# A bank of its own for the state products of a gated delta layer, and two output columns issued after the last head's sums

## The chip, the cores and the metric

One core of a Trainium2 chip runs the whole program. The metric is device time in microseconds (us) of one execution, as a median over several runs.

## What is computed

The program is a small network of three blocks on 512 tokens of width 1024. The change touches the first alone: a gated delta-rule layer with 8 heads of width 128, computed in chunks of 64 tokens. Cut to what matters:

```python
h = modulated_norm(x); proj = h @ w_in            # q, k, v, z: 4 x 8 column blocks of 128
# per head, chunks of 64: solve (I + L) [u, w] = [beta v, beta k exp(g)], L strictly lower triangular
def step(S, inp):                                 # 8 chunks, one after the other
    v_new = u_i - w_i @ S
    o = q_i @ S + a_i @ v_new
    S = S * gl_i + k_i.T @ v_new
    return S, o
o = rms(o) * silu(z)                              # per head
x = x + gate * (o.reshape(T, 8 * 128) @ w_out)    # output projection over all heads
```

Then follow a second attention layer and a third block with attention, an mLSTM and a mixture of experts. All matmuls of projections are done three times with operands split into a high and a low part (`mm3`, lines 106 to 108).

## The kernel before

A scheduler orders each engine's instructions from the program text, with its own estimate of times; each engine then works through its queue strictly in that order. What stands where is therefore read from the built order, and a change in one place can move instructions in others.

**Projections.** `proj_T` makes one column block of 128 outputs for all 512 tokens: per block of 128 inputs three matmuls of 128x512 (L106 to L108). The weights come from memory, ScalarE rounds them to the high part `wh` (L99), and the low part `wl` is subtracted on GpSimd or VectorE (L102). Which of the two is chosen in `wtile` by a running number, `self.uid`, that every buffer request counts up: VectorE where it divides by 9, else GpSimd.

**A head** (`gdn_head`). Its front transposes k and v and builds L. The solve runs five levels; each is a transpose (L611), a product with the masked L (L616; GpSimd makes the mask product `Lm`, L607) and a second product (L621). These, and the products u (L628) and w (L632), go through PSUM bank `v0` or `v1`, by the head's parity. The chain of 8 chunks then works in bank `s0` or `s1`, 512 columns in four quarters: R, the product with the state (L646), is read by VectorE to update u (L647) and by ScalarE to copy the inter-chunk output (L648); pS, the state product (L650), is read by VectorE to make the next state (L655). After the chain come the sums (L658: a product of A and u), the norm over the head (ScalarE, VectorE, GpSimd L123 and L668), transposes of the result (L670) and the product with silu(z) into `oT` (L671), which is split into `oH` and `oL` (L99, L102).

**The output projection** (`residual`) runs in two parts, `EARLY_A`: for all 8 column blocks first the heads 0 to 6 (7 input blocks, 21 matmuls a column), then head 7 alone (3 matmuls a column). After each, VectorE adds the column (L300); after the last part squares are summed for the next norm (L198, L114, a power on GpSimd at L123).

**Beside it.** Rows of the modulation (`ada`) are multiplied and summed in the head loop: the first two on VectorE in one instruction (L173), the others on GpSimd and ScalarE (L176, L177).

Of the kernel before, what the change touches and what calls it, by code (L numbers as in the profile page):

```python
# [19 lines left out]
P = 128  # L20
T = 512
D = 1024
KC = D // P
# [10 lines left out]
class Net:  # L34
# [251 lines left out]
                         w16[0][:, k], w16[1][:, k], k == 0, k == KC - 1)  # L286
        cb(p[:, :NT * 16].rearrange("p (i c) -> p i c", i=NT))

    def residual(self, w, act, gate, x_in, x_out, scratch=None, parts=(slice(0, KC),)):

        nc = self.nc
        held = {}

        def cb(j, p, first, last):
            src = x_in(j) if first else held.pop(j)
            out = x_out[:, j] if last else src
            if gate is None:
                nc.vector.tensor_tensor(out, src, p, op=ALU.add)
            else:
                nc.vector.scalar_tensor_tensor(out, p, gate[:, j:j + 1], src, op0=ALU.mult, op1=ALU.add)  # L300
            held[j] = out
            if last:
                held["sq"] = self.square(out, src if scratch is None else scratch(j), held.get("sq"), nc.vector)
        for ks in parts:
            self.proj_T(w, 0, KC, act, lambda j, p: cb(j, p, ks is parts[0], ks is parts[-1]), ks=ks)
        self.uid += 1
        self.rms = self.mean([held["sq"]], f"x{self.uid}")

# [18 lines left out]
class Gdn(Net):  # L327
# [9 lines left out]
    def gdn(self):  # L337
        nc, tc, a = self.nc, self.tc, self.a
# [4 lines left out]
        with ExitStack() as st:  # L343
# [8 lines left out]
            act = (hH, hL)  # L352
            w = a["w_in_a"]
            rts = ExitStack()
            rt = rts.enter_context(tc.tile_pool(name="g_rt", bufs=1))
            with tc.tile_pool(name="g_t", bufs=2) as tmp, tc.tile_pool(name="g_ada0", bufs=self.A0) as ap0:
# [11 lines left out]
                parts = {}  # L368
# [128 lines left out]
            oH = hp.tile([P, KC, T], F32R, tag="hH", name="oH")  # L497
            oL = hp.tile([P, KC, T], F32R, tag="hL", name="oL")
# [10 lines left out]
            class Out:  # L509

                def __getitem__(_, at):
                    if not x1:
                        x1[0] = self.xtile("x1")
                    return x1[0][at]
            self.residual(a["w_out_a"], (oH, oL), self.mod0[:, 16:24], x_in, Out(), parts=self.EARLY_A)
            x1 = x1[0]
            self.dump("x1", x1)
        return x1
# [7 lines left out]
    def gdn_head(self, hd, h, q, k, v, z, gcol, rows, oT):  # L526
        nc = self.nc
        dcm, strm, lvs, lv0t = self.masks
        mm = nc.tensor.matmul
# [28 lines left out]
        p = self.pg()  # L558
# [6 lines left out]
        A, B = late("A", [NT, P], 3), new("B", [NT, P], 2)  # L565
# [5 lines left out]
        for i2 in range(0, NT, 2):  # L571
            p = self.pg().rearrange("p (i a c) -> p i a c", i=2, a=2)
# [14 lines left out]
        p = self.pg()  # L587
# [5 lines left out]
        p = self.pg()  # L593
# [31 lines left out]
        u = late("u", [NT, P], 2)  # L625
        p = self.pg()
# [3 lines left out]
        p = self.pg()  # L630
# [5 lines left out]

        o = late("ot", [NT, P], 2)
        nc.gpsimd.memset(o[:64, 0], 0.0)
        ps = self.pg(f"s{h % 2}")
        S = None  # L640
        for c in range(T // 64):
            i, b = divmod(c, 2)
            pr, qr = slice(b * 64, b * 64 + 64), slice(64 - b * 64, 128 - b * 64)
            R, pS = ps[:, b * 256:b * 256 + P], ps[:, b * 256 + P:b * 256 + 256]
            if S is not None:
                mm(R, WQ[:, i, b].rearrange("p a c -> p (a c)"), S, start=True, stop=True, skip_group_check=True)  # L646
                nc.vector.tensor_tensor(u[pr, i], u[pr, i], R[pr], op=ALU.subtract)  # L647
                nc.scalar.copy(o[pr, i], R[qr])  # L648
            if c < T // 64 - 1:
                mm(pS, kd[pr, i], u[pr, i], start=True, stop=True, skip_group_check=True)  # L650
                S2 = late(f"S{h % 2}", [P], 2)
                if S is None:
                    nc.vector.tensor_copy(S2, pS)
                else:
                    nc.vector.scalar_tensor_tensor(S2, S, gl[:, c:c + 1], pS, op0=ALU.mult, op1=ALU.add)  # L655
                S = S2
        for i in range(NT):
            mm(ps[:, i * P:(i + 1) * P], A[:, i], u[:, i], start=True, stop=True, skip_group_check=True)  # L658
        nc.vector.tensor_tensor(o, o, v4(ps), op=ALU.add)

        ss = late("ss", [NT], 2)
# [977 lines left out]
```

## Time and profile before

| | |
|---|---|
| median of 3 runs | 2809.9 us (2806.88 to 2825.23) |
| the profiled execution | 2808.36 us, span 2806.6 us |
| TensorE / VectorE / ScalarE / GpSimd busy over the span | 95% / 61% / 43% / 62% |
| granted TensorE clock, mean | 0.983 of full speed |
| first layer | to about 520 us; its head loop from about 60 to 440 us |
| second layer, third block, experts | to about 900, 1510 and 2806 us |

In the rows below, PE is TensorE's matmul, PEld its weight load, DVE VectorE, ACT ScalarE and POOL GpSimd. A timeline row gives start, duration, engine, line, operation, output<-inputs, shape and count; in brackets stands the idle time of the engine before it and what ended it. Equal instructions in a row are merged, and a tile's number is left out, so that heads are told apart by counting in the order of the program. A 128x128 product of 32-bit numbers shows as two matmuls.

### The profile page before, as it was taken

What the parts mean: (1) busy time and instruction counts of PE and PEld (TensorE: products, weight loads), DVE (VectorE), ACT (ScalarE), POOL (GpSimd) and SP (SyncE); (2) the same over time, 40 slices, a digit from 0 to 9 for tenths busy, and PEclk for the clock granted to TensorE, in tenths of its full rate; (3) what the DMA queues carried; (4) which work ended last, traced back from release to release, by engine and by line L of the source; (5) the groups of instructions that cost most, each with busy time, mean ns of one, the idle gap of its engine ahead of it and who ended that gap; (6) DMA issues with size and microseconds to landing.
All of it is one profiled execution on the core that took longest, in us unless ns stands there. A gap on an engine that the chain in (4) does not pass through costs nothing. (4 is left out here: it accounts for less than half of the span.)

```text
span 2806.6 us, 40394 instructions
## 1 busy us (share of the span) xinstructions
PE 2663.2 (95%) x14601; PEld 2262.4 (81%) x14601; DVE 1698.3 (61%) x3092; ACT 1209.0 (43%) x2505; POOL 1735.8 (62%) x1338
## 2 busy tenths in 40 slices
PE   6899998799998999999998999999999999999999
PEld 4787777697776877787777899999999977777777
DVE  7767774614445654222232697798876167678897
ACT  5566663636664454233333333434434333333332
POOL 4799983543232521444365368878788478887886
PEclk9999999899998999999999999999999999999999
DMA  6243331221011111212122478888888889999996
GB/s 241 95 139 121 121 113 32 71 98 61 29 42 50 61 37 55 74 62 75 61 86 87 136 264 292 305 293 317 314 289 309 279 289 333 339 331 334 334 324 226
DMA packets 206793, 499.35 MB, mean 178 GB/s; under 512 B 18304, under 2 KB 106624, under 8 KB 203520
## 3 DMA queue, kind: packets, MB, share of 16 engines
q1 hardware_dynamic: 167856, 359.19, 38.0%
q0 software_dynamic: 36864, 134.23, 13.4%
q10 hardware_dynamic: 1872, 3.33, 0.4%
q8 instruction: 115, 1.88, 0.3%
q14 instruction: 86, 0.70, 0.1%
HBM read 444.26 MB, written 52.43 MB: 177 GB/s over the span
## 5 line engine op out<-in xcount | busy, mean ns | idle before, releaser
L102 POOL TENSOR_TENSOR wl<-wr,wh 128x256 fp32r<-128x256 f32 (+2 forms) x503 | 418.0, 850 | 493.1 <-ACT wh L99 466.0
L102 POOL TENSOR_TENSOR upl<-upr,uph 128x1024 fp32r<-128x1024 f32 x128 | 311.9, 2437 | 97.0 <-ACT uph L99 96.0
L99 ACT ACTIVATE wh<-wr 128x256 fp32r<-128x256 f32 (+2 forms) x556 | 228.4, 445 | 305.0 <-PE pj L107 114.5
L106 PE MATMUL pj<-nH,downh 128*128 128x384 f32 x1024 | 353.4, 345 | 2.4 <-ACT w L1458 1.3
L108 PE MATMUL pj<-nH,downl 128*128 128x384 f32 x1024 | 350.0, 342 | 2.7 <-DVE downl L102 2.7
L107 PE MATMUL pj<-nL,downh 128*128 128x384 f32 x1024 | 349.9, 342 | 0.0
L102 POOL TENSOR_TENSOR downl<-downr,downh 128x1024 fp32r<-128x1024 f32 x96 | 238.1, 2482 | 134.0 <-ACT downh L99 132.9
L1503 PE MATMUL acc<-uph,wwh 128*128 128x512 f32 x768 | 302.4, 399 | 8.9 <-ACT wwh L99 8.9
L1503 PE MATMUL acc<-upl,wwh 128*128 128x512 f32 x768 | 305.8, 398 | 0.0
L99 ACT ACTIVATE downh<-downr 128x1024 fp32r<-128x1024 f32 x128 | 135.4, 1059 | 312.5 <-PE pj L107 188.9
L102 DVE TENSOR_TENSOR wwl<-wo,wwh 128x384 fp32r<-128x384 f32 x128 | 210.8, 1650 | 58.0 <-ACT wwh L99 54.6
L1503 PE MATMUL acc<-uph,wwl 128*128 128x512 f32 x768 | 232.6, 399 | 5.6 <-DVE wwl L102 5.4
L106 PE MATMUL pj<-hH,wh 128*128 128x512 f32 x544 | 219.9, 404 | 2.2 <-ACT mo L1175 1.2
L108 PE MATMUL pj<-hH,wl 128*128 128x512 f32 x544 | 221.1, 407 | 0.3 <-POOL wl L102 0.2
L107 PE MATMUL pj<-hL,wh 128*128 128x512 f32 x544 | 215.3, 396 | 0.0
L99 ACT ACTIVATE uph<-upr 128x1024 fp32r<-128x1024 f32 x128 | 134.8, 1053 | 168.9 <-POOL upl L102 114.2
L106 PEld LDWEIGHTS pj<-nH,downh 128*128 128x128 f32 x1024 | 193.8, 189 | 5.4 <-ACT downh L99 1.6
L108 PEld LDWEIGHTS pj<-nH,downl 128*128 128x128 f32 x1024 | 194.0, 189 | 3.9 <-DVE downl L102 3.6
L107 PEld LDWEIGHTS pj<-nL,downh 128*128 128x128 f32 x1024 | 193.8, 189 | 0.3
L1503 PEld LDWEIGHTS acc<-uph,wwh 128*128 128x128 f32 x768 | 145.1, 189 | 47.7 <-ACT wwh L99 12.8
L1503 PEld LDWEIGHTS acc<-uph,wwl 128*128 128x128 f32 x768 | 145.0, 189 | 42.8 <-DVE wwl L102 7.8
L1503 PEld LDWEIGHTS acc<-upl,wwh 128*128 128x128 f32 x768 | 145.8, 190 | 35.0
(627 smaller groups left out, 6583.2 us busy)
## 6 DMA issues: line engine op xcount, KB each, us to landing
downr<-in_peer_down_j SPq DMA_DIRECT2D x128, 512.0 KB, 4.9
upr<-in_peer_up_j SPq DMA_DIRECT2D x128, 512.0 KB, 5.7
wr<-in_w_in SPq DMA_DIRECT2D x50, 512.0 KB, 4.1
ada<-in_w_ada SPq DMA_DIRECT2D x48, 512.0 KB, 3.8
wait<-w SPq DMA_DIRECT2D x128, 192.0 KB, 4.8
wo<-wait SPq DMA_DIRECT2D x128, 192.0 KB, 5.1
G<-stage SPq DMA_DIRECT2D x24, 1024.0 KB, 7.5
Gt<-G SPq DMA_DIRECT2D x48, 512.0 KB, 8.0
```

Of the source, the lines that this page charges most:

```text
L99: nc.scalar.activation(h, src, AF.Copy)
L102: return (eb or nc.vector).tensor_tensor(l, src, h.bitcast(F32), op=ALU.subtract)
L106: mm(out, lh, rh, start=start, stop=False)
L107: mm(out, lh, rl, start=False, stop=False)
L108: mm(out, ll, rh, start=False, stop=stop)
L1503: mm(po[z][b], lh[:, zs], rh[:, bs], start=False, stop=j == P - 1 and rh is uh and lh is l, skip_group_check=True)
```

## The change

pS moves from the quarter beside R to a bank requested by `self.pg()`, which is the head's own solve bank (`v0` or `v1`), still the tag in force there. R and pS now take the four quarters of their banks in turn. In `residual`, the last two column blocks of the first part are issued behind the last sums matmul of the last head (an edge in TensorE's order, no semaphore); the other six are left to the scheduler.

```diff
-    def residual(self, w, act, gate, x_in, x_out, scratch=None, parts=(slice(0, KC),)):
+    def residual(self, w, act, gate, x_in, x_out, scratch=None, parts=(slice(0, KC),), keep=(0, None)):
...
         for ks in parts:
-            self.proj_T(w, 0, KC, act, lambda j, p: cb(j, p, ks is parts[0], ks is parts[-1]), ks=ks)
+            n = KC - keep[0] if ks is parts[0] else KC
+            self.proj_T(w, 0, n, act, lambda j, p: cb(j, p, ks is parts[0], ks is parts[-1]), ks=ks)
+            if n < KC:
+                with self.tc.issue_after(keep[1].ins):
+                    self.proj_T(w, n, KC - n, act, lambda j, p: cb(n + j, p, ks is parts[0], ks is parts[-1]), ks=ks)
...
-            self.residual(a["w_out_a"], (oH, oL), self.mod0[:, 16:24], x_in, Out(), parts=self.EARLY_A)
+            self.residual(a["w_out_a"], (oH, oL), self.mod0[:, 16:24], x_in, Out(), parts=self.EARLY_A, keep=(2, self.summed))
...
-        ps = self.pg(f"s{h % 2}")
+
+        ps, pS2 = self.pg(f"s{h % 2}"), self.pg()
...
-            R, pS = ps[:, b * 256:b * 256 + P], ps[:, b * 256 + P:b * 256 + 256]
+            R, pS = (p[:, c % 4 * P:c % 4 * P + P] for p in (ps, pS2))
...
-            mm(ps[:, i * P:(i + 1) * P], A[:, i], u[:, i], start=True, stop=True, skip_group_check=True)
+            self.summed = mm(ps[:, i * P:(i + 1) * P], A[:, i], u[:, i], start=True, stop=True, skip_group_check=True)
```

Two things follow from the text without standing in it. The new buffer counts `self.uid` up once more per head, so other weight blocks fall to VectorE: of 556 weight splits 53 stood on VectorE, now 113 do. In the head loop these are 4 column blocks instead of 2, in the third block 10 pairs of blocks instead of 3 (8 splits each); the second pair of the second layer goes from VectorE to GpSimd, with its first split ahead of the rsqrt of that layer's norm. And lines from 289 on have higher numbers in the changed kernel: L646 becomes L652, L650 L656, L658 L664, L670 L676.

First place: TensorE at the end of head 5's chain (tiles s1 and, in the changed kernel, v1; u5, kd5), where head 7's solve (Xv17, Lmv17) begins beside head 6's (v0). Before:

```order
L650 MATMUL s1257_3405<-u5_3389,kd5_3177 128x128 [waits Activation_49]
L616 MATMUL v1314_4286<-Xv17_4278,Lmv17_4284 128x128 [waits Pool_49]
L616 MATMUL v1314_4286<-Xv17_4278,Lmv17_4284 128x128 x3
L611 MATMUL v0290_3877<-c_id_74,Xv06_3868 128x128 [waits DVE_49]
L611 MATMUL v0290_3877<-c_id_74,Xv06_3868 128x128 x3
L646 MATMUL s1257_3405<-S15_3443,WQ5_3231 128x128 [waits DVE_49]
```

Now:

```order
L656 MATMUL v1263_3411<-u5_3394,kd5_3182 128x128 [waits DVE_49]
L652 MATMUL s1262_3410<-S15_3449,WQ5_3236 128x128 [waits DVE_49,Activation_49]
L626 MATMUL v0298_3897<-Yv06_3895,XTv06_3888 128x128 [waits Activation_49]
L626 MATMUL v0298_3897<-Yv06_3895,XTv06_3888 128x128 x3
L621 MATMUL v1321_4293<-Xv17_4285,Lmv17_4291 128x128 x4
L664 MATMUL s1262_3410<-u5_3394,A5_3214 128x128 [waits Activation_49]
```

The state product waits for VectorE in place of ScalarE, and head 7's first solve product stands behind the whole of head 5's chain, just ahead of its sums.

Second place: TensorE around the last head's sums (A7), with columns of the output projection (pj). Before:

```order
L107 MATMUL pj348_4777<-oL_4500,wh348_4798 128x512
L108 MATMUL pj348_4777<-oH_4499,wl348_4799 128x512
L658 MATMUL s1334_4431<-u7_4415,A7_4237 128x128 [waits Activation_49]
L658 MATMUL s1334_4431<-u7_4415,A7_4237 128x128 x3
L106 MATMUL pj348_4777<-oH_4499,wh348_4808 128x512 [waits Activation_49]
```

Now:

```order
L656 MATMUL v1342_4439<-u7_4422,kd7_4212 128x128 [waits DVE_49]
L108 MATMUL pj354_4742<-oH_4507,wl354_4774 128x512 [waits Pool_49]
L652 MATMUL s1341_4438<-S17_4465,WQ7_4266 128x128 [waits DVE_49,Activation_49]
L656 MATMUL v1342_4439<-u7_4422,kd7_4212 128x128 [waits DVE_49]
L652 MATMUL s1341_4438<-S17_4471,WQ7_4266 128x128 [waits DVE_49,Activation_49]
L656 MATMUL v1342_4439<-u7_4422,kd7_4212 128x128 [waits DVE_49]
L652 MATMUL s1341_4438<-S17_4477,WQ7_4266 128x128 [waits DVE_49,Activation_49]
L664 MATMUL s1341_4438<-u7_4422,A7_4244 128x128 [waits Activation_49]
L664 MATMUL s1341_4438<-u7_4422,A7_4244 128x128 x3
L106 MATMUL pj356_4785<-oH_4507,wh356_4786 128x512
```

The last three chunks of the chain have no projection between them any more; the two columns held back (pj356, pj358) follow the sums, 21 and 8 matmuls ahead of the last transposes (L676) and 13 behind them; before, 3 and 21 stood between sums and transposes, and none of the first part behind these.

Third place: GpSimd early in the head loop, with the mask products of head 1 (Xv11, XTv11, Lmv11) and head 0 (Lmv00), weight splits (wl) and a row of the modulation (ada51). Before:

```order
L601 TENSOR_TENSOR Xv11_1194<-B1_1154,c_lv0t_457 128x512
L102 TENSOR_TENSOR wl143_1937<-wr142_0_1933,wh143_1936 128x256
L102 TENSOR_TENSOR wl143_1947<-wr142_0_1933,wh143_1946 128x256
L602 TENSOR_TENSOR XTv11_1195<-Ls1_1192,c_lv0_445 128x512
L607 TENSOR_TENSOR Lmv11_1200<-Ls1_1192,c_lv1_447 128x512
L102 TENSOR_TENSOR wl143_1957<-wr142_0_1933,wh143_1956 128x256
L176 TENSOR_TENSOR ada51_761<-ada51_761,c_rep_118 128x1024
L102 TENSOR_TENSOR wl143_1967<-wr142_0_1933,wh143_1966 128x256
L607 TENSOR_TENSOR Lmv00_763<-Ls0_682,c_lv4_453 128x512
```

Now:

```order
L606 TENSOR_TENSOR Xv11_1195<-B1_1155,c_lv0t_457 128x512
L102 TENSOR_TENSOR wl146_1940<-wr145_0_1936,wh146_1939 128x256
L102 TENSOR_TENSOR wl146_1950<-wr145_0_1936,wh146_1949 128x256
L607 TENSOR_TENSOR XTv11_1196<-Ls1_1193,c_lv0_445 128x512
L612 TENSOR_TENSOR Lmv11_1201<-Ls1_1193,c_lv1_447 128x512
L102 TENSOR_TENSOR wl146_1960<-wr145_0_1936,wh146_1959 128x256
L612 TENSOR_TENSOR Lmv00_763<-Ls0_682,c_lv4_453 128x512
L176 TENSOR_TENSOR ada51_761<-ada51_761,c_rep_118 128x1024
```

Head 0's mask product of the fourth level (Lmv00) now stands ahead of the row of the modulation.

## Rows read from the trace of the kernel before

**Rows 1.** Busy time by stage: stretch, its length, then each engine, TensorE's clock, DMA.

```profile
60.00:440.00 380.00, 355.42 (x2162) 299.51 (x2161) 272.79 (x480) 242.61 (x625) 321.55 (x283) 0.99 0.34 111
...
457.00:469.00 12.00, 8.97 (x26) 6.47 (x27) 5.47 (x15) 3.01 (x11) 3.51 (x4) 0.57 0.00 0
```

**Rows 2.** Timeline, 457 to 461 us: two chunks of the last head's chain.

```profile
457.84 0.48 PE L650 MATMUL s<-u,kd 64*128 64x128 f32 x2 [2.22 <-ACT ot L648]
...
458.77 0.80 PE L646 MATMUL s<-S,WQ 128*128 128x128 f32 x2 [0.44 <-DVE S L655]
...
459.60 0.28 DVE L647 TENSOR_TENSOR u<-u,s 64x128 f32<-64x128 f32 x1 [0.22 <-PE s L646]
459.92 0.26 ACT L648 COPY ot<-s 64x128 f32<-64x128 f32 x1 [2.13 <-DVE u L647]
...
460.23 0.79 PE L650 MATMUL s<-u,kd 64*128 64x128 f32 x2 [0.67 <-ACT ot L648]
```

**Rows 3.** TensorE's waits, 60 to 440 us: total, times, longest.

```profile
PE s L650 <- ACT ot L648: 2.0, 2, 1.4
```

**Rows 4.** Timeline of TensorE: first solve products (L616) and last state products (L650).

```profile
183.95 1.16 PE L616 MATMUL v<-Xv,Lmv 128*128 128x128 f32 x8
...
207.68 0.71 PE L650 MATMUL s<-u,kd 64*128 64x128 f32 x4
...
328.47 1.06 PE L616 MATMUL v<-Xv,Lmv 128*128 128x128 f32 x8
...
344.06 0.48 PE L650 MATMUL s<-u,kd 64*128 64x128 f32 x2
...
423.29 1.16 PE L616 MATMUL v<-Xv,Lmv 128*128 128x128 f32 x8 [0.59 <-POOL Lmv L607]
```

**Rows 5.** Timeline from head 6's sums to the next layer's norm.

```profile
454.25 1.16 PE L658 MATMUL s<-u,A 128*128 128x128 f32 x8
...
463.57 1.22 PE L106 MATMUL pj<-oH,wh 128*128 128x512 f32 x2 [1.08 <-ACT oH L99]
...
494.12 1.05 PE L658 MATMUL s<-u,A 128*128 128x128 f32 x8
...
499.70 1.04 POOL L668 TENSOR_TENSOR ot<-ot,rv_o 128x512 f32<-128x512 f32 x1
...
499.83 0.39 PE L106 MATMUL pj<-oH,wh 128*128 128x512 f32 x1
500.06 0.39 PE L107 MATMUL pj<-oL,wh 128*128 128x512 f32 x1
...
500.79 0.66 PE L670 MATMUL s<-c_id,ot 128*128 128x128 f32 x4
...
504.45 1.41 DVE L300 SCALAR_TENSOR_TENSOR x<-pj,mods,xi 128x512 f32<-128x512 f32 x2 [0.83 <-PE pj L108]
...
513.75 6.36 POOL L102 TENSOR_TENSOR wl<-wr,wh 128x512 fp32r<-128x512 f32 x4 [4.36 <-ACT wh L99]
...
520.08 1.00 POOL L123 TENSOR_TENSOR rv_x<-rv_x,mhalf 128x4 f32<-128x4 f32 x1
```

**Rows 6.** Line L173's instructions from 60 us on; timeline, 129 to 135 us.

```profile
L173 DVE CUSTOM_DVE_ANT_0 ada<-ada,c_rep,cols x2: 1277/5776/10276, 106.8 to 122.5; 128x1024 f32<-128x1024 f32 x2
...
129.39 2.33 POOL L176 TENSOR_TENSOR ada<-ada,c_rep 128x1024 f32<-128x1024 f32 x1
...
134.07 1.11 PE L542 MATMUL n<-c_id,y 128*128 128x128 f32 x4 [8.15 <-DVE vb L591]
```

**Rows 7.** Groups of weight splits, 60 to 440 us; TensorE's waits, 900 to 1510 us.

```profile
L102 POOL TENSOR_TENSOR wl<-wr,wh 128x256 fp32r<-128x256 f32 (+1 forms) x114 | 91.9, 814 | 26.9 <-ACT wh L99 26.0 <-PE s L650 0.6
...
L102 DVE TENSOR_TENSOR wl<-wr,wh 128x256 fp32r<-128x256 f32 x8 | 5.0, 637 | 0.7 <-ACT wh L99 0.7
...
PE l L107 <- POOL wl L102: 0.4, 1, 0.4
```

## The prediction

> **What bounds the kernel now.** I read the page first, then the busy time by stage, then the first layer's waits, and last its timeline, since the change lies there. In the head loop (60 to 440 us) it is busy 355 of 380 us, GpSimd 322, VectorE 273, ScalarE 243 [rows 1]: four engines that feed each other, none with much room. At the end of the layer two heads are left without further input projections, TensorE runs short of work, and from 457 to 469 us the granted clock is 0.57 between its levels of 1.2 and 2.4 GHz, after the idle time before 457.84 [rows 1, 2]. From 469 us on matmuls of the output projection fill every wait. So the change can act on three things: waits inside the state chain, the seam between head 6 and head 7, and the end of the layer. The experts from 1510 us on have the same instructions in nearly the same order, and move only as a block.
>
> One chunk of the chain at 458 us, where nothing else is queued [rows 2]: the product with the state (L646) starts at 458.77; VectorE subtracts it from u at 459.60 for 0.28 us; ScalarE copies the other half at 459.92 for 0.26 us; only then, at 460.23, comes the next state product (L650). It needs u alone, but the trace names ScalarE's copy as its releaser, because both products stand in one bank. At 457.84 the same wait had cost 2.22 us.
>
> **The change part by part.** All sums go against the profiled run, 2808.4 us (span 2806.6). The median of the runs shown is 2809.9, 1.5 us above it and within their scatter.
>
> (a) *State product in the v bank.* In the order its wait changes from ScalarE to VectorE (first place shown). In the step above u ends at 459.88 and a release takes some 0.05 us (copy end 460.18, product 460.23), so a bare step falls by 0.30 us. The next L646 now waits for the copy, which has a whole state update to finish in. 48 such steps would be 14.4 us if all lay on the path; none if projections fill them. As idle TensorE time named after that copy the trace shows 2.0 us in the head loop [rows 3] and 2.22 + 0.67 us in the two steps of rows 2. I take -4 (0 to -14).
>
> (b) *The seam of heads 6 and 7.* Before, head 6's sums (L658) start at 454.25, after the last product of head 7's solve, and the output projection, which needs head 6's normalised output, resumes at 463.57, waiting for its split [rows 5]: 9.3 us with little for TensorE. Now chain 6 is done earlier and its sums stand ahead of head 7's last solve product and of its u and w, so about half of the wait runs under work that has to be done anyway. -5 (0 to -9.3).
>
> (c) *The v bank is held longer.* Head h+2 solves in the bank where head h's state products now stand until its chain ends. Before, head 2's first solve product is at 183.95 and head 0's last state product at 207.68 (with one of head 1), an overlap of 24 us that is no longer allowed; head 5 against head 3 overlaps by 16 us (328.47, 344.06); head 7 starts at 423.29, with no overlap left [rows 4]. TensorE's order fills the shift with projection columns, as long as there are some. By head 7 that cover is nearly gone: head 7's solve now stands behind all of head 5's chain (first place shown), and by counting rows some 3 us more matmul work is ahead of it. Lower bound 0, upper bound the 16 us of head 5 less 14 half steps at 0.30, thus 12. Row 423.29 (no overlap) is nearer to what decides: +4.
>
> (d) *Two columns behind the sums.* Before, 24 matmuls at 0.23 us from start to start (499.83, 500.06) lie between the last sums, 494.12, and the transposes, 500.79, and cover the norm, which ends with the product at 499.70 [rows 5]. Now 29 do, 6.7 us, still enough. But the columns held back are missing ahead of the sums: the last steps stand bare in the order (second place shown). A bare step is 0.93 us (457.84 to 458.77) plus 1.16 (458.77 to 459.88 and a release), 2.1 us. Three of them are 6.3 us with 1.6 us of matmuls, so 4.7 us idle. In return 13 matmuls, 3.0 us, move from before the transposes to after them, where they cover the way from the transposes to the first finished column: before 3.66 us (500.79 to 504.45), now some 0.7 + 3.0 + 0.9 = 4.6. Transposes 4.7 - 3.0 = 1.7 later, then 0.9: +2.6. If the bare steps hide in slack won at (b), it is -2.1; I keep +2.6.
>
> (e) *The rsqrt of the next norm.* On GpSimd four weight splits of the second layer, 6.36 us, stand before it and push it to 520.08 [rows 5]. Now a fifth (1.59 us) stands there, because the running number moved that block from VectorE to GpSimd. +1 (0 to +1.6).
>
> (f) *A stall at 122 us.* VectorE's multiply-and-sum of 1024 columns takes 1.28 us once and 10.28 us at 122.5, and TensorE idles 8.15 us behind it [rows 6]. GpSimd has a run of operations over the same time, the last of them to 131.72 (129.39 + 2.33), and VectorE ends about 1 us later, at 132.8: it got through when GpSimd stopped. In the new order a split mask product (Lm of head 0) stands ahead of the 2.33 us operation (third place shown); it must wait for a matmul that itself waits behind the stall, so GpSimd should stop 2.3 us sooner. -2 (0 to -8; a new stall of the same kind at the first of the two would cost up to +4).
>
> The Trainium skill (SBUF — State Buffer, section "Who interferes with whom") says that a VectorE instruction with two SBUF inputs and a GpSimd instruction that reads SBUF take the shared port in turn, and that the second to issue fully blocks until the first finishes. By that the multiply should have waited for one GpSimd operation; the trace shows it waiting out a run, 10.28 us. By the page alone (f) would be 0 and the sum 2807.
>
> (g) *Splits that change engines.* Two more projection columns, 8 splits, go from GpSimd (mean 0.81 us) to VectorE in the head loop [rows 7]. -6.5 if GpSimd bounded it, +6.5 if VectorE did at the same price each; TensorE's waits name neither, so 0. In the third layer 56 splits move likewise; TensorE's whole wait for a GpSimd split there is 0.4 us [rows 7]: 0, within 3 us for what the other order does.
>
> Sum: -4 - 5 + 4 + 2.6 + 1 - 2 = -3.4, thus 2805.0.
>
> **Rivals.** *The held bank bounds the layer* (slower). If the shift of (c) isn't filled, the solves of one parity run one after the other: head 5's 16 us go to head 7 and to the end, less 4 from faster steps, with (d) and (e) in full and nothing from (b): 2808.4 + 12 + 2.6 + 1 - 4 = 2820. For it: from head 5 on the order shows hardly any projection rows between chain and solve. Against: until then it shows them in full, and head 7 had no overlap before. It decides once head 7's solve starts after 435 us, 12 us later than in row 423.29.
>
> *Nothing on balance.* TensorE's queue is fixed, waits saved come back at the next fill, and the seam gains only what the bare steps lose: 2808.4, within 1.5. For it: 8.15 + 2.0 us is nearly all of the named idle time that is large.
>
> *More than forecast.* The seam goes in full, -9.3, the clock's dip (12 us at 0.57, some 5 us lost) goes with it, chain steps give -6, the stall -4, against +4 + 2.6 + 1: 2808.4 - 16.7 = 2792. For it: the dip follows the idle time that (a) and (b) remove. Against: the last bare steps are a new idle time.
>
> **How the numbers follow.** Chances: forecast (2799 to 2807) 0.40, nothing on balance 0.22, held bank 0.20, more 0.18. The range goes to both outer cases, 2791 to 2820; some 2 in 10 lies outside. A measurement of this kernel tells about 1% (28 us) from no change; only tails of the outer cases reach that: faster 0.02, same 0.95, slower 0.03.
>
> **What would show it.** In the changed profile: state products released by VectorE, hardly ever by the copy (a); less than 9 us from head 6's sums to the next full fill, and a shorter dip of the clock (b); head 7's first solve product just after head 5's last state product, at 424 to 430 us (c); some 5 us of idle TensorE right before the last sums and none right after the transposes (d); the rsqrt behind five splits (e); the long multiply at 8 us (f). The prediction is wrong if head 7's solve starts that late, if the stall grows, or if the third layer, which I price at nothing, moves by more than 3 us.

## The result, and the profile after

| | before | after |
|---|---|---|
| median (6 runs each, one chip) | 2810.33 us (2806.88 to 2825.23) | 2842.04 us (2825.99 to 2854.88) |
| ratio to before, 95% interval | | 1.0107 (1.0075 to 1.0139) |
| profiled execution, span | | 2840.86 us, 2839.1 us |
| granted TensorE clock, mean | | 0.977 |

The kernel became about 30 us slower; 2805 was forecast, with 2820 as the upper end. In the profiled executions two places hold nearly all of it: the first layer ends 16.0 us later (the rsqrt of the next norm, 520.08 and 536.12), and the attention of the second layer takes 12 us more.

Busy time by stage in the profile after, columns as in [rows 1] (stretch, length, PE, PEld, DVE, ACT, POOL, clock, DMA, GB/s):

```profile
60.00:440.00 380.00, 351.71 (x2056) 294.23 (x2055) 274.78 (x467) 234.56 (x604) 313.21 (x266) 0.96 0.34 110
440.00:457.00 17.00, 15.53 (x101) 14.05 (x101) 6.42 (x19) 7.01 (x21) 7.85 (x10) 0.87 0.12 35
457.00:469.00 12.00, 9.79 (x71) 8.34 (x71) 4.71 (x14) 3.64 (x9) 1.26 (x1) 1.00 0.03 13
```

The hole that stood at 457 to 469 us, with a clock of 0.57 [rows 1], is gone; the clock is low earlier instead, 0.68 from 420 to 440 us and 0.87 from 440 to 457. And in the head loop TensorE got through fewer instructions (2056 against 2162), at 0.96 instead of 0.99. TensorE's waits there, largest first:

```profile
PE s L652 <- DVE S L661: 10.2, 9, 3.8
PE v L656 <- DVE u L653: 6.5, 8, 1.8
PE v L616 <- DVE Xv L628: 3.4, 5, 1.7
```

State products (now L656) are released by VectorE's u, as the edit says; ScalarE's copy [rows 3] is named no more. In its place the chain itself is waited for, 10.2 + 6.5 us: fewer projections stand between its steps. All idle time of TensorE from 60 us to the rsqrt grew by only 4.5 us, though (41.6 to 46.1), since before it held the 8.15 us of [rows 6]. The rest of the 16.0 us goes with the clock: TensorE was busy at the lower of its two levels (1.2 GHz) for 38.5 us instead of 16.8. Matmuls of 128x512 follow one another after 0.43 us there (829.59 and 830.02 us in run 5) and after 0.23 us at the higher level, which makes some 10 us, an estimate. What the chain now waits for, the timeline of TensorE shows, where [rows 4] had the starts of the solves:

```profile
194.21 0.38 PE L652 MATMUL s<-S,WQ 128*128 128x128 f32 x2
194.43 0.83 PE L621 MATMUL v<-Xv,Lmv 128*128 128x128 f32 x6
...
346.45 0.39 PE L652 MATMUL s<-S,WQ 128*128 128x128 f32 x2
346.67 1.06 PE L621 MATMUL v<-Xv,Lmv 128*128 128x128 f32 x8
...
438.50 0.76 PE L652 MATMUL s<-S,WQ 128*128 128x128 f32 x2 [0.53 <-DVE S L661]
439.06 1.91 PE L626 MATMUL v<-Yv,XTv 128*128 128x128 f32 x8
440.76 1.92 PE L621 MATMUL v<-Xv,Lmv 128*128 128x128 f32 x8
```

Three times the last product of a chain with the state is followed by the solve of the head two further on: heads 0 and 2, 3 and 5, 5 and 7. The start of a head's solve, minus the start of that last product of the head two before it (us; negative means that the solve ran beside the chain):

| | head 2 | head 3 | head 4 | head 5 | head 6 | head 7 |
|---|---|---|---|---|---|---|
| before | -28.4 | +16.0 | +3.0 | -19.3 | -6.0 | -1.6 |
| after | +0.2 | +1.1 | +0.2 | +0.2 | +2.3 | +2.3 |

Now every solve from head 2 on begins just behind that product; before, four of them began ahead of it and two behind it. The seam and the end of the layer, against [rows 5]:

```profile
467.24 1.10 PE L664 MATMUL s<-u,A 128*128 128x128 f32 x8
...
475.73 0.73 PE L106 MATMUL pj<-oH,wh 128*128 128x512 f32 x2
...
501.30 0.49 PE L656 MATMUL v<-u,kd 64*128 64x128 f32 x2 [0.61 <-DVE u L653]
502.32 0.74 PE L652 MATMUL s<-S,WQ 128*128 128x128 f32 x2 [0.53 <-DVE S L661]
503.43 0.79 PE L656 MATMUL v<-u,kd 64*128 64x128 f32 x2 [0.37 <-DVE u L653]
504.75 0.76 PE L652 MATMUL s<-S,WQ 128*128 128x128 f32 x2 [0.53 <-DVE S L661]
506.19 2.07 PE L664 MATMUL s<-u,A 128*128 128x128 f32 x8 [0.67 <-ACT ot L654]
...
515.24 0.60 PE L676 MATMUL s<-c_id,ot 128*128 128x128 f32 x4
...
529.09 7.07 POOL L102 TENSOR_TENSOR wl<-wr,wh 128x512 fp32r<-128x512 f32 x5 [4.39 <-ACT wh L99]
536.12 1.01 POOL L123 TENSOR_TENSOR rv_x<-rv_x,mhalf 128x4 f32<-128x4 f32 x1
```

From head 6's sums to the next fill it is 8.5 us (9.3 before). These sums come 13.0 us later than before, and from them to the rsqrt it is 68.9 us (65.8). The bare last steps cost 2.7 us of idle time (the five brackets). The rsqrt stands behind five splits, at 536.12 instead of 520.08.

The second layer, where no line of the program was changed. First the attention of the profile after, from its first to its last logits, and TensorE's largest wait in it; then the same from the trace of before, where the stretch took 206.7 us (the row is rounded to whole us) and that wait stood at 1.2 us, once:

```profile
665.70:884.80 219.10, 201.26 (x1148) 155.56 (x1147) 92.57 (x140) 130.13 (x277) 64.24 (x51) 0.96 0.12 37
...
PE l L817 <- ACT sHb_b L99: 11.6, 5, 6.3
...
649.00:856.00 207.00, 199.36 (x1149) 152.44 (x1147) 93.00 (x140) 130.64 (x278) 60.86 (x51) 0.99 0.12 40
...
PE l L811 <- ACT sHb_b L99: 1.2, 1, 1.2
```

### The profile page after: what moved, and what is told of

It reads as the page before. It is cut to its first block, busy times and chain, and to the rows that moved or that the text cites. A ratio compares the mean times of both kernels' runs of the same rounds, so it can differ in the third digit from the quotient of the medians.

```text
span 2839.1 us, 40448 instructions
## 1 busy us (share of the span) xinstructions
PE 2674.8 (94%) x14601; PEld 2272.3 (80%) x14601; DVE 1716.4 (60%) x3152; ACT 1206.8 (43%) x2505; POOL 1703.4 (60%) x1278
## 5 line engine op out<-in xcount | busy, mean ns | idle before, releaser
L102 POOL TENSOR_TENSOR wl<-wr,wh 128x256 fp32r<-128x256 f32 (+2 forms) x443 | 379.5, 876 | 530.9 <-ACT wh L99 513.1
L1509 PEld LDWEIGHTS acc<-uph,wwh 128*128 128x128 f32 x768 | 145.2, 189 | 51.5 <-ACT wwh L99 16.6
```

The source lines that it names most:

```text
L102: return (eb or nc.vector).tensor_tensor(l, src, h.bitcast(F32), op=ALU.subtract)
L1509: mm(po[z][b], lh[:, zs], rh[:, bs], start=False, stop=j == P - 1 and rh is uh and lh is l, skip_group_check=True)
```

## The experiments

Each run is a kernel of its own, timed on one chip together with the kernel before; each ratio is to that. What makes a comparison clean here is the built order. In runs 1 and 6 to 18 the numbers were set so that the later layers keep the order of before: of TensorE's 11,069 matmuls there 2 to 27 stand elsewhere, against some 625 in the change and in run 5, so that little but the first layer is compared. (In run 1 it is 11 rows, and not "row for row" as its expectation says.) One trace sizes nothing under about 10 us: run 5 has the order of before in its first layer, row for row, and ended it at 529.14 instead of 520.08; TensorE was busy at the lower clock for 40.2 us there, as long as in the change. So the medians decide, and the traces say where.

**Which part of the change: runs 1 to 4.** Run 1 adds one number at the end of the first layer:

```diff
             x1 = x1[0]
+            self.uid += 1
```

> The changed kernel, with the running number raised by one more at the end of the first layer (8 heads plus 1 are 9, and every ninth number sends a weight split to VectorE), so that from the second layer on the splits fall to the same engines as before, and the order of every engine there is that of the kernel before, row for row; the first layer stays as changed. Theory N (the second layer lost 12 us because splits changed engines there): last finished block of x1 stays at 528 us, the second layer's attention falls from 219 to 207 us (before 206.7), the third layer is as before, total 2826 (2823 to 2829). Rival C (the second layer is slow for what the first hands over, such as queues or transfers that run later): it stays at 219 us, total 2840.

Measured: 2827.66 us, 1.0064 (1.0043 to 1.0086), 0.43% (12 us) less than the change. The second layer is back to 205.4 us, and the long wait with it (attention of run 1, then its waits):

```profile
671.40:876.80 205.40, 198.61 (x1148) 152.42 (x1147) 93.00 (x140) 130.64 (x277) 60.97 (x51) 0.99 0.12 40
...
PE l L818 <- ACT sHb_b L99: 1.2, 1, 1.2
```

Theory N's total and its attention hold. The last block of x1 came at 535.0 us, not at 528, in a trace with three VectorE stalls of 6 to 14 us. Run 2 takes the bank without counting it:

```diff
-        ps, pS2 = self.pg(f"s{h % 2}"), self.pg()
+        ps, bank = self.pg(f"s{h % 2}"), f"v{h % 2}"
+        pS2 = self.pp.tile([P, 512], F32, tag=bank, name=f"{bank}b{h}", bufs=1)
```

> The changed kernel, with the second bank taken without counting it in the running number, so that all splits fall to the engines they had before. Theory H (the v bank held through the chain makes the solves of one parity run after each other): head 7's solve still starts only after head 5's chain, later than 435 us, x1 ends at 524 to 530 us; second layer back at about 207 us; total 2822 to 2827. Rival S (in the first layer it is the eight more column blocks' splits on VectorE that lengthen the chain steps): x1 ends at 513 to 516 us, total 2808 to 2813.

Measured: 2834.81 us, 1.0092 (1.0066 to 1.0118), 8 us over the expected range. Head 7's solve starts at 435.4 us, as H said, and the last block of x1 comes at 522.6, just under its range; but the second layer's attention took 219.3 us here too, though every split is on its engine of before. TensorE's order of the later layers is not that of before: some 540 rows stand elsewhere. So theory N falls in the form that I gave it: not the engine of a split, but the order that the scheduler then builds is what costs. Run 3 is the numbers alone, in all layers:

```diff
         ps = self.pg(f"s{h % 2}")
+        self.uid += 1
```

> The kernel before, with the running number raised by one per head and nothing else: the same splits go to VectorE as in the changed kernel. Theory H with N: first layer within 3 us of before (x1 at 510 to 516 us), second layer's attention at 219 us, third about 1 us longer, total 2820 to 2825. Rival S: x1 at 525 us or later, total 2835 to 2842.

Measured: 2829.53 us, 1.0080 (1.0050 to 1.0110), 5 us over the expected range. In its trace, of the fastest of its four executions (2815.96 us), the first layer loses nothing (rsqrt at 515.47), and the second layer's attention takes 219.4 us. Run 4 is the `residual` part of the change alone:

> The kernel before, with the two columns of the output projection queued behind the last head's sums and nothing else (state products in the s bank, numbers as before). Prediction's step: 3 to 5 us of idle TensorE in the last steps, some of it given back behind the transposes, x1 ends 2.6 us later (0 to 5), total 2808 to 2814. Rival T (the columns kept back are what made the end of the layer late): x1 8 us later or more, total over 2817.

Measured: 2816.43 us, 1.0035 (1.0014 to 1.0055), 2 us over the expected range. The first layer's rsqrt is at 515.98, so the columns do no harm in that trace; the second layer's attention, again in another order, takes 215.9 us.

**The two halves apart: runs 5 to 8.** Run 5 changes the later order and nothing in the first layer:

```diff
             x1 = x1[0]
+            self.uid += 8
```

> The kernel before, with the running number raised by eight once, at the end of the first layer: there every engine's order is the same as before, row for row; from the second layer on the splits and the order are nearly those of the changed kernel. Theory O (the later layers lost their time to the order that the scheduler then made; the first run showed that with the old order it comes back): first layer as before, x1 at 505 to 513 us, second layer's attention at 217 to 220 us instead of 207, total 12 to 15 us over before, 2822 to 2826. Rival C (the later loss needs what the changed first layer hands over): attention at 207 us, total within 4 us of before.

Measured: 2829.75 us, 1.0059 (1.0036 to 1.0082): 16.6 us, a little over the 12 to 15 expected. Attention 222.4 us (217 to 220 expected), so nearly all of it lies there. The waits of that stretch, and TensorE's rows around the longest:

```profile
PE l L812 <- ACT sHb_b L99: 14.0, 4, 6.8
...
820.16 1.12 PE L791 MATMUL l<-q,kT 64*128 64x512 f32 x2
821.21 0.33 PE L794 MATMUL l<-cr_sbm,cr_id 128*128 128x128 f32 x1
821.37 0.45 PE L106 MATMUL pj<-oH,wh 128*128 128x512 f32 x1
821.66 0.39 PE L107 MATMUL pj<-oL,wh 128*128 128x512 f32 x1
821.88 0.40 PE L108 MATMUL pj<-oH,wl 128*128 128x512 f32 x1
829.11 0.69 PE L812 MATMUL l<-sHb_b,cr_nui 128*128 128x384 f32 x1 [6.82 <-ACT sHb_b L99]
829.59 0.63 PE L106 MATMUL pj<-oH,wh 128*128 128x512 f32 x1
```

This is the sixth of eight pairs. After a pair's logits, ScalarE needs some 8 us for the softplus of six tiles and the split `sHb_b`. TensorE bridges that with projection matmuls. Here three of them stand behind the logits and one between them; in the order of before (run 1's trace) 14 stand between the same pair's logits and 9 behind them, and the same wait is 1.22 us. Two other pairs got more of them (the third 62 half-size ones instead of 12 whole and 43 half-size, the fourth 4 and 48 instead of 23 and none); what covered one wait now stands at another. With the waits the granted clock falls (0.95 over the stretch against 0.99 in run 1): a matmul of 128x512 takes 0.63 us behind the wait, 0.39 ahead of it. Run 6 is the other half, the numbers in the first layer alone:

```diff
         ps = self.pg(f"s{h % 2}")
+        self.uid += 1
...
             x1 = x1[0]
+            self.uid += 1
```

> The kernel before, with the running number raised by one per head and by one more at the end of the first layer: only the first layer's splits move to VectorE as in the changed kernel, the order of the later layers is as before but for 18 rows of TensorE. Theory H: the moved splits cost the first layer nothing (0 to 4 us), total 2808 to 2814, and the 18 us of the run with the numbers set back belong to the bank and the columns. Rival S: the moved splits are a large part of them, total 2818 or more.

Measured: 2811.98 us, 1.0011 (0.9996 to 1.0026). The splits that move to VectorE cost the first layer nothing that can be seen. It is the control of runs 1 and 7, which have the two columns as well: adding these to run 6 leaves TensorE's built order the same, row for row. Run 7 is run 1 with the hold (the v bank stays taken until the chain ends) and nearly without the relief (a state product that no longer waits for ScalarE's copy):

```diff
-            R, pS = (p[:, c % 4 * P:c % 4 * P + P] for p in (ps, pS2))
+            R = ps[:, b * 256:b * 256 + P]
+            pS = pS2[:, c % 4 * P:c % 4 * P + P] if c == 6 else ps[:, b * 256 + P:b * 256 + 256]
```

> The changed kernel with the numbers set back for the later layers, in which only the last state product of a head goes to the v bank and the first six stay in the s bank as before: the v bank is still taken until the chain ends, while the steps keep ScalarE's copy as their releaser and the first product no longer waits for the two copies out of the w product. Theory H (the hold alone costs it): head 7's solve after 435 us, x1 at 523 us or later, total 2824 to 2832. Rival W (it is the first state product, which now stands behind the copies, that makes each head late): x1 at 508 to 514 us, total 2808 to 2816.

Measured: 2840.68 us, 1.0117 (1.0092 to 1.0142), 9 us over the expected range. Nearly alone, the hold costs 1.06% over its control, 30 us; run 1, which has the relief too, is 0.53%, 15 us, faster than it. The line-up in run 7's timeline, head 3's last product and head 5's solve:

```profile
365.72 0.39 PE L654 MATMUL s<-S,WQ 128*128 128x128 f32 x2
365.95 1.06 PE L622 MATMUL v<-Xv,Lmv 128*128 128x128 f32 x8
```

Run 8 puts only the first product into the v bank (as run 7's diff, with `c == 0`, on the kernel before):

> The kernel before, with only the first state product of each head in the v bank (numbers as before, later layers in the order of before but for 16 rows of TensorE): it waits for the two copies out of the w product, and the v bank is free again one copy later. Theory H: without the long hold little happens, x1 at 505 to 514 us, total 2808 to 2815. Rival W (about 4 us more per head between w and the first state product): 8 heads at 2 to 4 us, in part hidden, x1 at 518 us or later, total 2820 to 2830.

Measured: 2813.94 us, 1.0007 (0.9984 to 1.0030). Rival W, at 2820 or more, falls: the wait for the two copies out of w costs nothing that can be seen (the interval ends at 0.3%, 8 us).

**Is it the columns, the relief, or a draw of the order: runs 9 to 18.** The running number draws another order of the first layer with every value added per head, so the same edits were repeated in other numberings (m per head, and at the end what makes the sum a multiple of nine). Run 9 is the bank without columns, m = 2:

> State products in the v bank as in the changed kernel, no columns kept back; numbers raised in the first layer so that the order of the later layers is that of before but for 6 rows of TensorE. Theory H: the bank alone does the first layer's harm, total 2824 to 2831, head 7's solve after 435 us. Rival T (a part of the first layer's 17 us is the kept-back columns'): total 2818 or less.

Measured: 2818.18 us, 1.0027 (1.0005 to 1.0049); head 7's solve at 429.7 us, just behind head 5's last product with the state (429.5). By its letter rival T; without a control that was open. Run 10 is the columns in m = 7:

> The kernel before with the two columns behind the last head's sums, and numbers raised in the first layer so that the order of the later layers is that of before but for 6 rows of TensorE. Theory O: the 6 us of the columns' first run were the later order's (its second layer's attention took 216 us instead of 207), so total 2808 to 2814, attention at 207 us. Rival T: the columns cost it themselves, total 2816 or more. The prediction's step said 2.6 us.

Measured: 2818.34 us, 1.0033 (1.0016 to 1.0051), attention 208.3 us. By its letter T again. Run 11 moves the copy behind the product (m = 6):

```diff
-                nc.scalar.copy(o[pr, i], R[qr])
...
                 mm(pS, kd[pr, i], u[pr, i], start=True, stop=True, skip_group_check=True)
+                if c:
+                    nc.scalar.copy(o[pr, i], R[qr])
```

(the last step's copy in an `else`).

> The kernel before with ScalarE's copy of the product's other half written behind the next state product, so that this product waits for VectorE's u alone as in the changed kernel, but in the s bank, with no bank held longer; later layers in the order of before but for 12 rows. If steps without the copy are worth the 13 us by which the run with the hold and without the relief was slower than the one with both: total 2797 to 2804. If in the kernel before projections fill those steps anyway (the relief only shows where the hold has made the chain the bound): 2808 to 2814. Slower than 2815 if the copy, now behind the product in the same bank, delays the next one.

Measured: 2817.48 us, 1.0013 (0.9988 to 1.0038). In its trace the product is released by VectorE's u, as meant. No gain can be seen, and the 7 us or more of the first theory lie outside the interval. But m = 6 has no control, and one numbering cost 11 us by itself (below); so it is likely, not shown, that the copy costs nothing in the kernel before. By the median the run lies in the third range, over 2815. Then the controls (run 12: numbers alone, m = 2; run 14: m = 7; run 16: m = 4), bank and columns as in the change (run 13: m = 2; run 15: m = 4), and the hold without most of the relief (run 17: m = 2, first and last product in the v bank; run 18: m = 4, the last two). Their edits are the ones above with other numbers.

> Control of the run with the bank and no columns: the kernel before with the running number raised by two per head and by two at the end of the first layer, nothing else; later layers in the order of before but for 12 rows of TensorE (with the two columns kept back its order would be the same, row for row). Theory H: the moved splits cost nothing again, total 2808 to 2814, and the 7 us of the bank's run are the bank's. Rival D (each order that the scheduler draws for the first layer is worth several us either way, and the bank's 7 us are such a draw): 2816 or more.

> Bank and columns as in the changed kernel, with the numbers of the control above, 33 rows of TensorE away from the bank's run in the first layer. If the columns cost something on top of the bank: 2823 to 2830 (the 17 us of the run with the numbers set back). If the difference of 10 us between that run and the bank's was the numbers' draw of the order: 2815 to 2821.

> Control of the columns' second run: the kernel before with the running number raised by seven per head and at the end, no columns kept back; 46 rows of TensorE away from it in the first layer. If the columns cost 7 us: 2808 to 2814. If that was the draw of the order (or the stalls of the scatter): 2815 to 2821.

> Bank and columns as in the changed kernel in a third numbering (four per head, four at the end), later layers in the order of before but for 6 rows. Theory H: the held bank makes the first layer longer whatever the splits: head 7's solve late, total 2818 to 2832. Rival D: anywhere from 2805 up, below 2815 in one of the three numberings.

> Control of the third numbering: the kernel before with the running number raised by four per head and at the end of the first layer; later layers in the order of before but for 4 rows of TensorE. If the bank is dear in this numbering too: 2808 to 2814, against 2822 with bank and columns. If the 11 us there are the numbering's own: 2818 to 2824.

> The second numbering's run with bank and columns, in which only the first and the last state product of a head go to the v bank: the bank is taken as long, but five of seven steps keep ScalarE's copy as their releaser. Theory H with relief (two effects of opposite sign, as in the change's own numbering, where the hold without the relief was 29 us slower than its control and the relief took 13 off): 8 to 30 us over its control of 2815, so 2823 to 2845. Rival D (the 29 us were that numbering's draw): 2811 to 2819.

> The same in the third numbering, with the last two state products in the v bank and the first five in the s bank. Theory H with relief: over 2826, thus slower than bank and columns with the relief (2822), and 8 to 30 us over its control. Rival D: within 4 us of its control.

Measured, medians: run 12 2814.86 us, 13 2816.02, 14 2822.55, 15 2821.75, 16 2808.77, 17 2824.22, 18 2821.74. As ratios to before with their intervals:

| numbering | control | hold, (nearly) no relief | bank and columns | bank alone |
|---|---|---|---|---|
| m = 1 (the change's) | 1.0011 (0.9996, 1.0026) run 6 | 1.0117 (1.0092, 1.0142) run 7 | 1.0064 (1.0043, 1.0086) run 1 | |
| m = 2 | 1.0018 (0.9998, 1.0038) run 12 | 1.0052 (1.0033, 1.0070) run 17 | 1.0016 (0.9997, 1.0034) run 13 | 1.0027 (1.0005, 1.0049) run 9 |
| m = 4 | 1.0005 (0.9984, 1.0025) run 16 | 1.0054 (1.0032, 1.0077) run 18 | 1.0033 (1.0014, 1.0051) run 15 | |
| m = 7 | 1.0038 (1.0023, 1.0054) run 14 | | (columns alone) 1.0033, run 10 | |

Three readings. *Hold and relief are two effects of opposite sign.* In each row the hold is the slowest, by 1.06, 0.34 and 0.49% over its control (30, 10, 14 us), and the relief takes 0.53, 0.36 and 0.21% off (15, 10, 6 us). Net, the bank costs 0.53, -0.02 and 0.28%: 15, 0 and 8 us. In m = 2 and m = 4 the intervals of neighbouring cells touch or overlap; that the sequence is the same three times is what I rest on, and not the sizes, since hold and relief kernels of one numbering also differ in the order of 520 to 630 of TensorE's 1,936 rows of the first layer. (In m = 1 and m = 4 bank and columns come together, without a run of the bank alone.) Run 18 missed its 2826 by the median; the kernel before was 3 us faster on that chip, and the ratio is what counts. *The columns cost nothing that can be seen*: run 10 equals its control, run 13 is not slower than run 9, and in m = 1, 2 and 4 the control's order with the columns is the same, row for row. *A numbering is worth up to 11 us by itself* (m = 7), though 1 to 5 us in the other three. So rival D, in runs 12 to 18, is right about the size of the net loss (it depends on the drawn order) and wrong about the hold. Neither a version of the bank nor one of the columns came out faster than the kernel before.

What the hold forbids can be read from the traces, as the table above did for before and after (solve start minus the last product of the head two before, us):

| | head 2 | head 5 | head 7 |
|---|---|---|---|
| m = 1: control, hold | -28.2, +0.3 | -52.7, +0.2 | +3.7, +0.3 |
| m = 2: control, hold | -36.7, +0.2 | -17.9, +0.2 | -7.0, +0.2 |
| m = 4: control, hold | -36.0, +0.3 | -27.1, -1.0 | +1.0, +0.2 |

In every hold run the overlaps are gone. In the controls, head 5's differs most between the numberings, 53, 18 and 27 us, and stands in the order of the hold's cost, 30, 10 and 14 us. That is one trace each; that this overlap sets the price was not tried.

## Why the prediction was wrong

Of the 30 us by the ratio (31.7 by the medians), 18 are run 1's and 16.6 run 5's, each with an interval of some 6 us either way; their sum, 34.6, is met within those. Point by point:

- **The step that failed is (g), what other splits and the other order do to the later layers: 0, within 3 us.** I priced the splits by who waits for GpSimd, and only in the third layer. There it held: in the traces of before and after, the third block takes 2.5 us more (613.4 and 615.9 us between the rsqrts at its ends). But the second layer was in no term, and there TensorE's rows had been rearranged: 16.6 us (run 5). TensorE, VectorE and ScalarE have the same instructions in the attention (1148, 140 and 277 or 278 records); matmuls that covered ScalarE's softplus moved to pairs that were covered already. The rearranged rows stood in the built order before the forecast, and counting the projection matmuls at each pair's logits (at the sixth, 23 before, 6 in the change, 4 in run 5) would have shown it.
- **(c) was mis-sized, and (a) with it.** The line-up was seen, its price was not: +4 (0 to 12) against 30 us in this numbering, 10 and 14 in the others. The bound took one overlap, head 5's 16 us, as all that could be lost, and trusted the projections to fill the rest; but all six solves from head 2 on now stand in line, and in this numbering the overlap at head 5 that the hold forbids is 53 us, which the rows of the kernel before could not show. (a) was -4 (0 to -14): 15 us in this numbering, with the hold in place; without it run 11 showed no gain. Together they were forecast at 0 and are +15. The rival "held bank bounds the layer" had this right, with its threshold of 435 us, passed at 440.76, its sign and its layer: 2820 against run 1's 2828.
- **(b)** did not come: 8.5 us instead of 9.3 at the seam, the low clock earlier instead of shorter, and from head 6's sums to the rsqrt 3.0 us more than before, not 5 less. It wasn't tried alone.
- **(d)**: the bare steps came, with 2.7 us idle instead of 4.7; runs 10 and 13 show no price for the columns, though 2.6 us would not stand out from their intervals of some 5 us either way.
- **(e)** held: five splits, 7.07 us, and x1's last block to rsqrt 0.7 us longer (512.77 to 520.08, 528.07 to 536.12).
- **(f)** was no property of the kernel. The long multiply-sum [rows 6] did not come again in run 5, whose first layer has the order of before (1.52 us), nor in the change (2.40 us, not the 8 that were named as its sign), and came in run 13 (8.74 us); other instructions stalled in other executions (below). So 8 us of the profiled run of before were a draw, which I priced as if an edit could move it.

What stays open: whether the overlap at head 5 is what makes the hold cost 30 us in one numbering and 10 in another; and how much of either loss is waits and how much the clock that goes with them. In run 5's trace the second layer's wait grew by 12.8 us, and the time that TensorE was busy at the lower clock in that attention from 3.4 to 18.7 us. Over all executions the mean granted clock was 0.973 to 0.980 in the change, and 0.979 to 0.985 in the 15 executions of the kernel before that stand beside run 1.

## What to carry to other kernels

Where a scheduler orders the queues, compare the whole built order after an edit, not just the edited region: here about half of the loss sat in a layer that no line of the change touches, and it showed as a count of filler matmuls behind each group of logits. A separate buffer for a product is bought with the time that the buffer is held; look at who needs it next and chain the shifts over all its users before setting a price. And time an edit in a few equivalent variants of the order, since one variant here was worth up to 11 us by itself.

## What the hardware showed

Small VectorE instructions can stall for far longer than one GpSimd instruction. In run 10 one on 128x4 elements, 0.16 to 1.38 us at its seven other places in the trace, lasts 12.95 us, and VectorE has no other row meanwhile. From 142.01 us on eleven instructions of GpSimd stand without a pause; the last ends at 156.42, VectorE's at 156.45. VectorE's row, and GpSimd's first and last:

```profile
143.50 12.95 DVE L567 TENSOR_SCALAR cols<-rv_q 128x4 f32<-128x4 f32 x1
...
142.01 1.02 POOL L123 TENSOR_TENSOR rv_q<-rv_q,mhalf 128x4 f32<-128x4 f32 x1
...
154.09 2.33 POOL L176 TENSOR_TENSOR ada<-ada,c_rep 128x1024 f32<-128x1024 f32 x1
```

In run 16 the same instruction took 12.96 us, in run 1 a 128x1 sum 13.80 us. The Trainium skill (SBUF — State Buffer, section "Who interferes with whom") has the second to issue on the shared port pair block until the first finishes; that is one instruction, and these rows show a whole run of them, as [rows 6] did. That the port is the reason was not tried: by the same section an instruction with a single SBUF input, as the one of 12.95 us, contends only in a two-port mode, and no run shows its mode. Stalls explain the hold at most in part: in the head loop run 7's trace has two, of 5.2 and 3.7 us, its control, run 6, has none over 3 us, and their first layers end 24 us apart.

After the idle stretch of 6.82 us in run 5, TensorE's clock was not back at once. From 821.0 to 829.1 us the granted clock was 0.75; from 829.1 to 840.0 it was 0.72, though TensorE was busy for 10.89 of these 10.9 us; from 840 to 850 it was 1.00.
